# Row transfers of the scan stage: one merged transfer, or one per half of the partitions

## The chip, the cores and the metric

The kernel runs on one core of a Trainium2 chip, in one launch. The metric is the device time of the program in microseconds. Executions of the same kernel differ by some tenths of a per cent.

## What is computed

One step of a bidirectional diffusion backbone over 128 context and 1024 latent tokens of width 1024. The layer is a half-step SwiGLU network, a token mixer, and a second half-step SwiGLU network, each with norms and modulation around it. The mixer projects its input to r, k, v, a gate and the operands of a short convolution, runs an RWKV-7 scan (8 heads of 64) forward and backward, and merges the branches:

```
kk  = k * k_k;  kk = kk * rsqrt(sum_head(kk * kk))
k_d = k * (1 + (a_d - 1) * k_a)                      # one per direction d
S   = S * w_t + (S @ -kk_t) x (kk_t * a_t) + v_t x k_t
y_t = S @ r_t                                        # both directions are summed
bonus = sum_head(r * k_d * r_k)
out = merged(sigmoid(gates), y @ w_branch_a, conv @ w_branch_b) @ w_out
```

## The kernel before

All activations lie with features on the 128 partitions and 1152 tokens along the free axis, in three column tiles of 384. A float32 matmul is done as three products of rounded halves (hi and lo). The first SwiGLU network takes the time up to about 930 us, the mixer's scan stage reaches to about 2130 us, and the output projections and the second network come after it.

In the scan stage, heads are taken two at a time: a pair p has head 0 on partitions 0 to 63 and head 1 on partitions 64 to 127. Operands of the scan are kept in device memory in `ops2`, one tile for two pairs, of shape 128 partitions x 9 rows x 2 pairs x 1152 tokens; `opd[p]` is the part of pair p. The rows are read by the scan as five neighbours per direction in one transfer (`stage_b`, L1017, the tile ops). For this to give each engine its operands on the right partitions, some quantities lie in different rows for the two heads: k in rows 5 (head 0) and 4 (head 1), kk in rows 4 and 5, and the factors of k for the two directions in rows 2 and 1, and 7 and 6. The function `mirrored` (L772) builds the access pattern of such a quantity by hand, as two heads of 64 partitions with a step of one row between them, so that one transfer carries both.

Who uses it:

- `k_to_dram` (L778) stores each of the 12 projected k tiles, 128 x 384, 192 KB. Its `store` puts the transfer on a list that `stores` (L713) issues six dense steps later.
- `stage_k` (L943) runs 20 times, 16 for 256 columns and 4 for 128. It loads k (tile ok, L949), the two factors (tiles od and oi, L952 and L953), all merged, and r plainly (L1002). Then it makes kk (L971), with a sum of squares on PE (tile cps) and an inverse root of small DVE steps (tiles nx, ny, nt), stores kk merged (L972), and loads v and stores the bonus term (L962, L980, the tensor bvd).

All of these transfers, and the weight loads (`load_w`, L151, the tile wst), are issued by SP, one after another in the program's order; an issue that has to wait for something holds up what is behind it.

Three lanes of side work (`stage_k`, `stage_v`, `finish`) are advanced between the matmuls of the projections; priorities and a scheduler's estimates set the order on every engine. The scan itself goes by items: `stage_b` loads the operands and makes the products (tile scr on PE), `solve` inverts a triangular block on DVE (tiles un, tb, ys, xr; copies to ab), `step` advances the states. Each of the 18 items has such a solve.

Of the kernel before, what the change touches and what calls it, by code (L numbers as in the profile page):

```python
# [22 lines left out]
T = NCTX + NLAT  # L23
# [3 lines left out]
TW = T // NT  # L27
# [33 lines left out]
def body(ctx: ExitStack, tc: tile.TileContext, I: dict, y_prompt, y_sample, new_state):  # L61
# [393 lines left out]
    with ExitStack() as ph:  # L455
# [123 lines left out]
        later.add(x_rest())  # L579
        ffn(ap_, op_, sp, I["ffn1_w13"][0], I["ffn1_w2"][0], [(0,), (1,), (2,)], between, done, None, w0)  # L580
        mix = mixer(nc, tc, pool, locals())
        next(mix)
        later.flush()
# [75 lines left out]
def mixer(nc, tc, pool, env):  # L659
# [4 lines left out]
    V, G, S, PE, SP, I = e.V, e.G, e.S, e.PE, e.SP, e.I  # L664
# [3 lines left out]
    after, PB, later = e.after, e.PB, e.later  # L668
    ops2 = e.ops2
    opd, vd, bvd, gd, gad, gbd, yad, cbvd, xd = e.opd, e.vd, e.bvd, e.gd, e.gad, e.gbd, e.yad, e.cbvd, e.xd  # L670
# [38 lines left out]
    def store(dst, src):  # L709

        late.append((dst, src, clock["dense"]))
# [59 lines left out]

    def mirrored(p, row, sign, t0, n):  # L772

        t_ = ops2[p // 2]
        ps = 18 * T
        return bass.AP(tensor=t_.tensor, offset=t_.offset + 2 * row * T + p % 2 * T + t0, ap=[[64 * ps + 2 * sign * T, 2], [ps, 64], [1, n]])

    def k_to_dram(p):  # L778
        def f(t, ps):
            o = e.tmp("fso", tag="s")  # L780
            PB.first(S.activation(out=o, in_=ps, func=AF.Copy))
            store(mirrored(p, 5, -1, t * TW, TW), o)
        return f

    made = set()
# [14 lines left out]
    with ExitStack() as ph:  # L800
# [16 lines left out]
        HR = [slice(0, 64), slice(64, 128)]  # L817
# [125 lines left out]
        def stage_k(p, t0, n, bon=True):  # L943

            while ("rkv", p) not in made:
                yield 1
            nt = n // 128
            k = q1.tile([128, 256], F32, name="ok", tag="ok")[:, :n]
            PB.first(SP.dma_start(k, mirrored(p, 5, -1, t0, n)))  # L949
            r = oload(opd[p][:, 3], t0, n, "or")  # L950
            f0, f1 = (q1.tile([128, 256], F32, name=f"o{x}", tag=f"o{x}")[:, :n] for x in "di")
            SP.dma_start(f0, mirrored(p, 2, -1, t0, n))  # L952
            SP.dma_start(f1, mirrored(p, 7, -1, t0, n))  # L953
            yield GL
            a = q1.tile([128, 256], F32, name="oa", tag="oa")[:, :n]
            PB.first(S.activation(out=a, in_=k, func=AF.Square, scale=e.KK_[:, p:p + 1]))
            b = f0
            PB.first(V.tensor_tensor(out=b, in0=f0, in1=f1, op=ALU.add))
            V.tensor_tensor(out=b, in0=b, in1=k, op=ALU.mult)
            V.scalar_tensor_tensor(out=b, in0=r, scalar=rk4[:, p:p + 1], in1=b, op0=ALU.mult, op1=ALU.mult)  # L960
            v = r
            SP.dma_start(v, vd[p][:, t0:t0 + n])  # L962
            yield 3
            rs = compact(a, nt, sel, 2, 1.0, 1e-12, "oc", PB)
            yield GC
            ps = ps_.tile([128, 256], F32, name="kkb", tag="oc", bufs=1)[:, :n]
            for i in range(nt):
                for h in range(2):
                    PB.matmul(ps[HR[h], i * 128:(i + 1) * 128], rs[:, 2 * i + h:2 * i + h + 1].to_broadcast([128, 64]), ident, start=True, stop=True)
            kk = a  # L970
            V.scalar_tensor_tensor(out=kk, in0=k, scalar=e.KK_[:, p:p + 1], in1=ps, op0=ALU.mult, op1=ALU.mult)  # L971
            SP.dma_start(mirrored(p, 4, 1, t0, n), kk)  # L972
            made.add(("kk", p, (t0 - NCTX) // 256))
            yield 4
            ps = ps_.tile([128, 256], F32, name="bon", tag="oc", bufs=1)[:, :n]
            PB.matmul(ps, bones, b, start=True, stop=True)
            o = v
            V.tensor_tensor(out=o, in0=v, in1=ps, op=ALU.mult)
            S.activation(out=o, in_=o, func=AF.Identity, bias=gb4[:, p:p + 1])
            SP.dma_start(bvd[p][:, t0:t0 + n], o)  # L980
            yield GF

        def stage_v(p, t0, n, zv):


            nb = n // 64
            while ("rkv", p) not in made:
                yield 1
            v = oload(vd[p], t0, n, "lv", PB.first)
            yield GL  # L990
            ps = ps_.tile([128, 4, 64], F32, name="vt", tag="oc", bufs=1)
            for i in range(nb):
                for h in range(2):
                    hr, kr = HR[h], HR[1 - h]
                    PB.matmul(ps[kr, i], v[hr, i * 64:i * 64 + 64], cent[hr] if t0 >= NCTX else ident[hr, hr], start=True, stop=True)
            for h in range(2):
                S.activation(out=zv[HR[1 - h], 0:nb, p % 2, HR[h]], in_=ps[HR[1 - h], 0:nb], func=AF.Copy)
            made.add(("vt", p, (t0 - NCTX) // 256))

        def oload(src, t0, n, tag, first=lambda ins: None):  # L1000
            a = q1.tile([128, 256], F32, name=tag, tag=tag)[:, :n]
            first(SP.dma_start(a, src[:, t0:t0 + n]))  # L1002
            return a
# [327 lines left out]
        def ks(g, *bs):  # L1331
            return [("k", stage_k, 2 * g + pp, NCTX + b * 256, 256) for pp in range(2) for b in bs]

        def vs(g, *bs):
            return [("v", stage_v, 2 * g + pp, NCTX + b * 256, 256, ZV[zi(g, b)]) for b in bs for pp in range(2)]
# [4 lines left out]
        def kc(q):  # L1340
            return [("k", stage_k, 2 * q + pp, 0, 128) for pp in range(2)]

        def vc(q):
            return [("v", stage_v, 2 * q + pp, 0, 128, ZV[(0, 3)[q]]) for pp in range(2)]
# [90 lines left out]
    with ExitStack() as ph:  # L1435
# [47 lines left out]
        for t in range(NT):  # L1483
            xs = hx(t)
            for m in range(8):
                w = load_w(I["w_out"][0, :, m * 128:(m + 1) * 128], 8)
                ps = pd("po")
# [31 lines left out]
```

## Time and profile before

| | |
|---|---|
| median of 3 runs | 3277.09 us (3270.9 to 3281.26) |
| profiled execution | 3285.59 us, span 3283.8 us |
| mean granted TensorE clock | 0.951 |
| PE busy | 3023.5 us (92%) |
| DVE busy | 1817.5 us (55%) |
| ACT busy | 1150.9 us (35%) |
| queue of SP's transfers | 480248 packets, 326.79 MB, 33.4% of 16 engines |

The busy times and the queue are those of the profiled execution. A share of the DMA engines is a mean over all 16 of them: a transfer that uses two of them all the time gives some 0.13. The chain of waits is followed back from the last instruction, at each step to what released it; a piece of it that bears a transfer's name runs from the issue to the landing on which something waited.

### The profile page before, as it was taken

Reading aid. Unit: us, or ns where it says so; the run is one execution under the profiler, and the core shown is the slowest. Engines: PE = TensorE matmul, PEld = TensorE weight load, DVE = VectorE, ACT = ScalarE, POOL = GpSimd, SP = SyncE. Lnnn points to the kernel's source line nnn. Section 1 sums busy time; section 2 is a strip of 40 time slices with the busy share of each in tenths; the row PEclk is TensorE's granted clock in tenths of the full one; section 3 lists DMA queues with packets and bytes.
Section 4 is the critical chain, followed back from the end, with each engine's and each line's share of the span. In section 5 each row is a group of like instructions: output and inputs, shape, how many; then the busy total and the mean of one; then the engine's idle time right before and its main releaser. Section 6 shows DMA issues by size and latency. Waiting matters only on the chain.

```text
span 3283.8 us, 54891 instructions
## 1 busy us (share of the span) xinstructions
PE 3023.5 (92%) x21284; PEld 2850.2 (87%) x21284; DVE 1817.5 (55%) x4148; ACT 1150.9 (35%) x2618; POOL 454.6 (14%) x436
## 2 busy tenths in 40 slices
PE   8999999999989878888889898769989999999998
PEld 5999999999888867767777777649989999999998
DVE  7535665565875244557674667766683233323356
ACT  5421111114546224344544444422554211121244
POOL 1000000000240121333331323200120000000012
PEclk9999999999989988988999889869999999999999
DMA  8423333325534331322232333225532111111244
GB/s 270 144 63 95 97 102 87 86 85 153 157 109 162 125 118 58 110 76 78 81 111 84 98 87 98 85 78 157 178 104 87 36 46 43 44 39 42 82 144 132
DMA packets 481137, 330.78 MB, mean 101 GB/s; under 512 B 47008, under 2 KB 458988, under 8 KB 480876
## 3 DMA queue, kind: packets, MB, share of 16 engines
q1 hardware_dynamic: 480248, 326.79, 33.4%
q8 instruction: 167, 2.74, 0.3%
q14 instruction: 94, 0.77, 0.1%
q10 hardware_dynamic: 308, 0.44, 0.0%
q0 software_dynamic: 320, 0.04, 0.0%
HBM read 265.58 MB, written 61.60 MB: 100 GB/s over the span
## 4 chain that ended last, share of the span: by engine, by line
PE 68%; DVE 17%; DMA 6%; ACT 4%; issue 3%; POOL 1%; SPq 0%; DVEq 0%; ACTq 0%; POOLq 0%
PE po L220 6%; PE po L219 6%; PE po L221 6%; PE pg L220 5%; PE pg L219 5%; PE pg L221 5%; PE pu L220 5%; PE pu L219 5%; PE pu L221 5%; PE pj L740 3%; PE pj L742 2%; PE pj L741 2%; DVE un L1084 2%; PE scr L1043 2%; DMA ops<-opd 2%
## 5 line engine op out<-in xcount | busy, mean ns | idle before, releaser
L138 ACT ACTIVATE whi<-wst 128x512 fp32r<-128x512 f32 (+1 forms) x578 | 350.4, 611 | 753.1 <-PE po L221 392.8
L139 DVE TENSOR_TENSOR wlo<-wst,whi 128x512 fp32r<-128x512 f32 (+1 forms) x480 | 326.6, 681 | 305.2 <-ACT whi L138 295.7
L740 PE MATMUL pj<-hh,wlo 128*128 128x384 f32 x1056 | 382.2, 362 | 0.3 <-ACT fso L768 0.3
L741 PE MATMUL pj<-hl,whi 128*128 128x384 f32 x1056 | 372.7, 353 | 2.7 <-POOL hl L269 1.4
L742 PE MATMUL pj<-hh,whi 128*128 128x384 f32 x1056 | 374.6, 355 | 0.0
L219 PE MATMUL po<-ah,wlo 128*128 128x384 f32 x1056 | 357.1, 339 | 4.0 <-ACT ah L138 4.0
L220 PE MATMUL pg<-hl,whi 128*128 128x384 f32 x1056 | 356.1, 337 | 4.9 <-POOL hl L269 2.9
L219 PE MATMUL pg<-hh,wlo 128*128 128x384 f32 x1056 | 357.4, 338 | 1.7 <-DVE wlo L139 1.3
L220 PE MATMUL po<-al,whi 128*128 128x384 f32 x1056 | 356.3, 338 | 0.4 <-DVE al L139 0.4
L221 PE MATMUL po<-ah,whi 128*128 128x384 f32 x1056 | 355.7, 337 | 0.0
L221 PE MATMUL pg<-hh,whi 128*128 128x384 f32 x1056 | 355.5, 337 | 0.0
L219 PE MATMUL pu<-hh,wlo 128*128 128x384 f32 x1056 | 355.2, 336 | 0.0
L220 PE MATMUL pu<-hl,whi 128*128 128x384 f32 x1056 | 353.8, 335 | 0.0
L221 PE MATMUL pu<-hh,whi 128*128 128x384 f32 x1056 | 353.8, 335 | 0.0
L279 POOL TENSOR_TENSOR ss<-ss,sqt 128x384 f32<-128x384 f32 x78 | 88.7, 1140 | 1697.0 <-ACT sqt L278 1534.9
L432 DVE TENSOR_TENSOR sil<-sil,pu 128x384 f32<-128x384 f32 x132 | 72.9, 552 | 353.8 <-PE pu L221 353.6
L404 DVE TENSOR_TENSOR o<-o,po 128x384 f32<-128x384 f32 x288 | 159.2, 553 | 172.0 <-PE po L221 170.8
L740 PEld LDWEIGHTS pj<-hh,wlo 128*128 128x128 f32 x1056 | 206.4, 195 | 12.5 <-issue 7.0
L741 PEld LDWEIGHTS pj<-hl,whi 128*128 128x128 f32 x1056 | 207.1, 196 | 8.6 <-issue 2.2
L742 PEld LDWEIGHTS pj<-hh,whi 128*128 128x128 f32 x1056 | 206.9, 196 | 7.6 <-issue 3.7
L220 PEld LDWEIGHTS pg<-hl,whi 128*128 128x128 f32 x1056 | 199.9, 189 | 7.0 <-POOL hl L269 3.8
L219 PEld LDWEIGHTS po<-ah,wlo 128*128 128x128 f32 x1056 | 198.6, 188 | 5.0 <-ACT ah L138 5.0
(584 smaller groups left out, 5763.9 us busy)
## 6 DMA issues: line engine op xcount, KB each, us to landing
wst<-in_ffn_w SPq DMA_DIRECT2D x324, 256.0 KB
wmod<-in_w_mod SPq DMA_DIRECT2D x144, 256.0 KB
wst<-in_w_in SPq DMA_DIRECT2D x94, 256.0 KB
ops<-opd SPq DMA_DIRECT2D x36, 640.0 KB
wst<-in_ffn_w SPq DMA_DIRECT2D x96, 192.0 KB
xo<-xd SPq DMA_DIRECT2D x64, 192.0 KB
wst<-in_w_out SPq DMA_DIRECT2D x48, 256.0 KB
opd<-zv SPq DMA_DIRECT2D x24, 384.0 KB
```

What stands on the lines that cost most here:

```text
L138: first(S.activation(out=hi, in_=src, func=AF.Copy))
L139: eng.tensor_tensor(out=lo, in0=src, in1=hi.bitcast(F32), op=ALU.subtract)
L219: PE.matmul(ps, lo, xh, start=(k == 0), stop=False)
L220: PE.matmul(ps, hi, xl, start=False, stop=False)
L221: later.tick(PE.matmul(ps, hi, xh, start=False, stop=(k == nk - 1)))
L279: eng.tensor_tensor(out=ssum, in0=ssum, in1=q, op=ALU.add)
L404: V.tensor_tensor(out=O[m][t], in0=O[m][t], in1=ps, op=ALU.add)
L432: V.tensor_tensor(out=s, in0=s, in1=pu, op=ALU.mult)
L740: PE.matmul(ps, lo, xh, start=(k == 0), stop=False)
L741: PE.matmul(ps, hi, xl, start=False, stop=False)
L742: ins = PE.matmul(ps, hi, xh, start=False, stop=(k == 7))
L1043: PE.matmul(ps[64 * o:64 * o + 64, i], BK[64 * h:64 * h + 64, o, i * 64:i * 64 + 64], E[64 * h:64 * h + 64, s0 + i, h], start=True, stop=True)
```

## The change

`mirrored` returns two plain patterns, one per head, of 64 partitions and one row each. Each load and each store that used the merged pattern is issued twice, for the upper and the lower half of the tile. 80 transfers of `stage_k` and 12 of `k_to_dram` become 184. The computation stays.

```diff
--- before.py
+++ after.py
@@ -771,15 +771,14 @@
 
     def mirrored(p, row, sign, t0, n):
 
-        t_ = ops2[p // 2]
-        ps = 18 * T
-        return bass.AP(tensor=t_.tensor, offset=t_.offset + 2 * row * T + p % 2 * T + t0, ap=[[64 * ps + 2 * sign * T, 2], [ps, 64], [1, n]])
+        return [opd[p][64 * h:64 * h + 64, row + sign * h, t0:t0 + n] for h in range(2)]
 
     def k_to_dram(p):
         def f(t, ps):
             o = e.tmp("fso", tag="s")
             PB.first(S.activation(out=o, in_=ps, func=AF.Copy))
-            store(mirrored(p, 5, -1, t * TW, TW), o)
+            for h, dst in enumerate(mirrored(p, 5, -1, t * TW, TW)):
+                store(dst, o[64 * h:64 * h + 64])
         return f
 
     made = set()
@@ -946,11 +945,11 @@
                 yield 1
             nt = n // 128
             k = q1.tile([128, 256], F32, name="ok", tag="ok")[:, :n]
-            PB.first(SP.dma_start(k, mirrored(p, 5, -1, t0, n)))
+            turned(k, mirrored(p, 5, -1, t0, n), PB.first)
             r = oload(opd[p][:, 3], t0, n, "or")
             f0, f1 = (q1.tile([128, 256], F32, name=f"o{x}", tag=f"o{x}")[:, :n] for x in "di")
-            SP.dma_start(f0, mirrored(p, 2, -1, t0, n))
-            SP.dma_start(f1, mirrored(p, 7, -1, t0, n))
+            turned(f0, mirrored(p, 2, -1, t0, n))
+            turned(f1, mirrored(p, 7, -1, t0, n))
             yield GL
             a = q1.tile([128, 256], F32, name="oa", tag="oa")[:, :n]
             PB.first(S.activation(out=a, in_=k, func=AF.Square, scale=e.KK_[:, p:p + 1]))
@@ -969,7 +968,8 @@
                     PB.matmul(ps[HR[h], i * 128:(i + 1) * 128], rs[:, 2 * i + h:2 * i + h + 1].to_broadcast([128, 64]), ident, start=True, stop=True)
             kk = a
             V.scalar_tensor_tensor(out=kk, in0=k, scalar=e.KK_[:, p:p + 1], in1=ps, op0=ALU.mult, op1=ALU.mult)
-            SP.dma_start(mirrored(p, 4, 1, t0, n), kk)
+            for h, dst in enumerate(mirrored(p, 4, 1, t0, n)):
+                SP.dma_start(dst, kk[HR[h]])
             made.add(("kk", p, (t0 - NCTX) // 256))
             yield 4
             ps = ps_.tile([128, 256], F32, name="bon", tag="oc", bufs=1)[:, :n]
@@ -996,6 +996,10 @@
             for h in range(2):
                 S.activation(out=zv[HR[1 - h], 0:nb, p % 2, HR[h]], in_=ps[HR[1 - h], 0:nb], func=AF.Copy)
             made.add(("vt", p, (t0 - NCTX) // 256))
+
+        def turned(dst, srcs, first=lambda ins: None):
+            for h, src in enumerate(srcs):
+                first(SP.dma_start(dst[HR[h]], src))
 
         def oload(src, t0, n, tag, first=lambda ins: None):
             a = q1.tile([128, 256], F32, name=tag, tag=tag)[:, :n]
```

The scheduler places the other instructions anew. On SP, at the operands of the first item, the program of before has (lines of before; opd_110 is the tile of pairs 0 and 1, opd_111 that of pairs 2 and 3):

```order
L1234 DMA sti<-in_state_rwkv 128x2x64
L972 DMA opd_110<-oa 2x64x256
L716 DMA opd_111<-fso 2x64x384
L952 DMA od<-opd_110 128x1x256
L1017 DMA ops<-opd_110 128x10x128
L980 DMA bvd_117<-or 128x256
```

In the changed program the same place reads (L1021 is the former L1017, L1002 the loads in the new function `turned`, L1238 the former L1234):

```order
L1238 DMA sti<-in_state_rwkv 128x2x64
L716 DMA opd_111<-fso 64x384
L972 DMA opd_110<-oa 64x256 x2
L716 DMA opd_111<-fso 64x384 x2
L1002 DMA od<-opd_110 64x256 x2
L1021 DMA ops<-opd_110 128x10x128
L980 DMA bvd_117<-or 128x256
```

Each merged transfer is a pair there; halves of k stores stand on both sides of the kk pair, and the pair is still followed by the od load and the ops load.

On DVE, at the end of an early solve, the program of before has, from the first transpose of the solve to its two last copies (od is the bonus product, nx the start of the inverse root):

```order
L1104 STREAM_TRANSPOSE xr<-ys 128x256
L958 TENSOR_TENSOR od<-od,oi 128x256
L1105 STREAM_TRANSPOSE xr<-xr 128x256
L959 TENSOR_TENSOR od<-od,ok 128x256
L960 SCALAR_TENSOR_TENSOR od<-or,rk_9040,od 128x256
L1126 COPY ab_11542<-l64b 32x4x32
L1126 COPY ab_11543<-l64b 32x4x32
```

In the changed program, from the same transpose on:

```order
L1108 STREAM_TRANSPOSE xr<-ys 128x256
L958 TENSOR_TENSOR od<-od,ok 128x256
L1109 STREAM_TRANSPOSE xr<-xr 128x256
L959 SCALAR_TENSOR_TENSOR od<-or,rk_9040,od 128x256
L238 TENSOR_SCALAR nx<-cps 128x4
L229 TENSOR_SCALAR ny<-nx 128x4
L231 SCALAR_TENSOR_TENSOR nt<-ny 128x4
L232 TENSOR_TENSOR nt<-nt,nx 128x4
L233 SCALAR_TENSOR_TENSOR ny<-nt,ny 128x4
```

The copies to ab come after these rows and four more of the same root; at two more of the 18 solves rows of stage_k moved ahead of the copies in the same way.

## Rows read from the trace of the kernel before

**Rows 1.** Busy time by stage: us, busy us (instructions) per engine, clock, DMA share, GB/s.

```profile
0.00:930.00 930.00, 899.81 (x5097) 873.38 (x5098) 565.04 (x1078) 281.37 (x585) 58.89 (x61) 0.99 0.41 120
930.00:2130.00 1200.00, 1031.19 (x9727) 902.18 (x9727) 703.24 (x1954) 516.12 (x1336) 319.37 (x304) 0.91 0.33 100
2130.00:3283.80 1153.80, 1092.47 (x6468) 1074.63 (x6464) 549.23 (x1117) 353.40 (x698) 76.33 (x71) 0.96 0.29 86
```

**Rows 2.** Chain of waits from 930 to 2130 us: its shares by engine and line.

```profile
by line: PE pj L740 6.9%; PE pj L742 6.7%; PE pj L741 6.6%; issue 5.8%; DVE un L1084 5.7%; PE scr L1043 5.0%; DMA ops<-opd 4.6%; DMA opd<-oa 2.3%; DVE tb L1085 2.1%; DMA od<-opd 2.0%; DVE e L1036 1.9%; DMA bvd<-or 1.8%; PE sq L1161 1.7%; DV
```

**Rows 3.** Longest pieces of the whole chain: start us, us, what.

```profile
1077.28 6.95 DMA wst<-in_w_in
1085.31 9.49 DMA bvd<-or
1098.50 8.50 DMA wst<-in_w_in
1146.38 6.22 DMA opd<-oa
1152.62 8.49 DMA ops<-opd
...
1268.88 6.13 DMA lv<-vd
...
1307.57 5.86 DMA ok<-opd
...
1598.61 9.30 DMA od<-opd
1649.43 10.14 DMA od<-opd
```

**Rows 4.** Two pieces of the same chain with nothing in the way.

```profile
1000.80 2.70 DMA opd<-zv
...
1416.52 4.22 DMA ops<-opd
```

**Rows 5.** Stretches with one kind of transfer in flight; columns as in rows 1.

```profile
977.00:978.40 1.40, 1.40 (x10) 1.40 (x9) 1.10 (x1) 0.49 (x1) 0.02 (x1) 1.00 0.69 177
1150.00:1152.00 2.00, 2.00 (x14) 2.00 (x13) 0.00 (x0) 0.53 (x2) 1.91 (x2) 1.00 0.14 49
1657.50:1659.00 1.50, 1.50 (x11) 1.50 (x10) 1.43 (x3) 0.49 (x1) 0.00 (x0) 1.00 0.14 49
```

**Rows 6.** PE in order of time: start us, us, line, tiles; in brackets idle before.

```profile
1097.83 0.33 PE L740 MATMUL pj<-hh,wlo 128*128 128x384 f32 x1
1098.01 0.33 PE L741 MATMUL pj<-hl,whi 128*128 128x384 f32 x1
...
1107.59 1.01 PE L177 MATMUL cps<-cst,oa 128*128 128x2 f32 x4 [9.08 <-ACT oa L956]
...
1110.21 0.52 PE L742 MATMUL pj<-hh,whi 128*128 128x384 f32 x1
1110.53 0.52 PE L740 MATMUL pj<-hh,wlo 128*128 128x384 f32 x1
...
1163.61 0.69 PE L1043 MATMUL scr<-e,ops 64*64 64x128 f32 x4 [9.38 <-DVE ops L1032]
...
1609.66 0.32 PE L1112 MATMUL l<-xr,ab 32*32 32x32 f32 x4 [6.79 <-DVE nt L231]
```

**Rows 7.** SP's issues by source line: count, ns least/median/most, first and last start.

```profile
L972 SPq DMA_DIRECT2D opd<-oa x20: 492/517/533, 1081.8 to 2046.7; - x20
...
L1002 SPq DMA_DIRECT2D or<-opd x20: 319/329/464, 935.3 to 2014.7; - x20
...
L882 SPq DMA_DIRECT2D lw<-in_decay_w x2: 497/526/554, 975.7 to 982.9; - x2
...
L980 SPq DMA_DIRECT2D bvd<-or x20: 320/729/3842, 1085.3 to 2058.3; - x20
```

**Rows 8.** Waits of DVE, 930 to 2130 us: us in total, times, longest.

```profile
DVE nx L238 <- PE cps L177: 37.9, 20, 6.9
```


## Prediction

> **What bounds the kernel now.** I read the busy time by stage first, to see where an idle engine costs time [rows 1]. The kernel is matmul work: before 930 us PE is busy 899.81 of 930.00 us, after 2130 us 1092.47 of 1153.80. In between lies the scan stage, where every split transfer of the change stands, and there PE is busy 1031.19 of 1200.00 us: 169 us idle, more than in all the rest, and the granted clock is 0.91 against 0.99 and 0.96. PE's instructions stand in a fixed order, scan work and projections mixed, so the change can shorten the kernel only by shortening these waits (or by giving clock back).
>
> Then I read the chain of waits in that stage [rows 2]. Four names of transfers stand in its line: ops<-opd 4.6%, opd<-oa 2.3%, od<-opd 2.0%, bvd<-or 1.8% of 1200 us, so 55.2, 27.6, 24.0 and 21.6 us. opd<-oa is the merged kk store, od<-opd a merged load. The other two are plain transfers that run behind merged ones. The longest pieces of the chain say the same [rows 3]: a merged load of 128 KB takes 9.30 or 10.14 us, a merged store of 128 KB 6.22 us, plain transfers queued behind them 9.49 (bvd), 8.49 (ops) and 6.95 and 8.50 us (wst). Where nothing is in the way, the plain store opd<-zv of 384 KB takes 2.70 us and the 640 KB load of ops 4.22 us [rows 4].
>
> Why a merged transfer is slow is told by the share of the 16 DMA engines [rows 5]. From 1150 to 1152 us one merged od load moves alone: the share is 0.14, some two engines of sixteen, at 49 GB/s, and from 1657.5 to 1659 us again 0.14 and 49 GB/s. At that rate 128 KB take 2.7 us and the 192 KB of a k store 4.0 us. From 977.0 to 978.4 us the 64-partition loads of lora weights (L882, L883) move: share 0.69, 177 GB/s. So 64 rows are no hindrance to using most of the engines; the merged form is. 64 merged transfers of 128 KB, 16 of 64 KB and 12 of 192 KB keep these two engines busy for 64 x 2.7 + 16 x 1.3 + 12 x 4.0 = 242 us, and every other transfer has a part on them and lands only when that part does.
>
> The Trainium skill gives the same reading in "DMA: Bandwidth & Descriptors", "Why a DMA increments its semaphore by 16 and not by 1": the number of engines is the largest up to 16 that divides the slowest dimension of both patterns. By that rule the merged pattern, whose slowest dimension is 2, gets 2 engines and a half of 64 rows gets 16; the trace agrees for the merged form (0.14) and nearly for the 64-row loads (0.69).
>
> **The change part by part.** 20 rounds of stage_k (16 of 256 columns, 4 of 128) issue 4 merged transfers each, and 12 k stores stand beside them: 92 transfers become 184. The bytes stay.
>
> *Landing times.* I price each piece of the chain at what the same or a larger transfer takes when nothing is in the way, plus the issue of the second half (0.33 us, below) for the split ones. ops, 10 pieces: 55.2 - 10 x 4.22 = 13.0. kk store, 5 pieces: 27.6 - 5 x 3.03 = 12.5. od, 3 pieces: 24.0 - 3 x 3.03 = 14.9. bvd, 3 pieces: 21.6 - 3 x 2.70 = 13.5. The two wst pieces at no less than ops: 15.45 - 8.44 = 7.0. lv 6.13 - 2.70 = 3.4, ok 5.86 - 3.03 = 2.8 [rows 2 to 4]. Together 67 us of the chain.
>
> *How much of that PE feels.* Four places can be followed [rows 3, 6]. At 1107.59 us PE resumes after 9.08 us; bvd and wst would give 6.8 + 4.3 there, so the whole 9.0. At 1163.61 us it resumes after 9.38; kk store and ops give 3.2 + 4.3 = 7.5. At 1609.66 us after 6.79; od gives 6.3. But behind the longest piece, the od load of 1649.43 us, PE is busy 1.50 of 1.50 us between 1657.5 and 1659 [rows 5]: projections fill it, and the 7.1 us there buy nothing. So 22.8 of 32.0 us are felt, 71%. I take that share for the stage: 47 us.
>
> *SP's issue time.* A merged transfer costs SP 0.517 us to issue, a plain one of 128 rows and 256 columns 0.329, and the trace has no 64-row transfer of plain form; the 64-row load L882, whose rows are in four pieces, takes 0.526 [rows 7]. A half has one run per row like the plain one, so I take 0.33; then a pair costs 0.66 - 0.517 = 0.14 more, 13 us over 92. With 0.526 it is 0.54 more, 49 us. Against it, bvd's store, which stands behind a merged transfer, takes 0.729 in the median and up to 3.842 us to issue, where 0.32 is its least: some 8 us of SP over its 20 issues that should come back. SP mostly waits for data, so I put 5 us of the added issue on the path. Lower end: nothing, if the returned issue time outweighs it; upper end: half of 49, 24 us.
>
> *Order.* On SP the halves stand as pairs where the merged one stood, and the kk pair is still directly ahead of the od pair and the ops load. What is queued behind a waiting half is the same as before, plus the other half. On DVE the order moved at three of 18 solves: there some eight rows more of stage_k's inverse root (from nx on) stand between the solve's transposes and its last copies (ab<-l64b), and nx waits for PE 37.9 us over 20 times, 1.9 us each [rows 8]. Three such waits ahead of a solve's end: 6 us. Lower bound 0, where the solve is late anyway.
>
> *Sum.* -47 + 5 + 6 = -36 us. The profiled execution took 3285.6 us (span 3283.8 and 1.8 around it), 8.5 above the median of the runs shown, 3277.1; I take the difference to that median: 3241 us. Left out on purpose: clock. Before the gap at 1107.59 us matmuls follow each other by 0.18 us, after it by 0.32, half the clock, 1.2 instead of 2.4 GHz [rows 6]. Shorter gaps might save some of that, 8 us at most (about 1.5 us at each of five or so long gaps).
>
> **The rivals.**
>
> *The whole chain is felt.* What the projections fill now is run earlier, so the end moves by all 67 us plus the 8 of clock: -75, 3202 us. For it: these pieces are on the path that sets the end, and behind ops, the name with most pieces, stands scr, at which PE's order stops until it has come [rows 6]. Against: PE busy behind the 10.14 us piece.
>
> *Hidden anyway.* The solve's DVE chain and the inverse roots are next late at most places, and only the two gaps above 9 us shrink by half: -8, 3269 us. For it: nx and its like wait for PE themselves. Against: PE's gaps at three followed places begin and end with a transfer.
>
> *Slower, by SP's queue.* SP issues in order, and in a round four pairs stand ahead of the ops and weight loads. If a half costs 0.526 us to issue and lands no sooner than now, each round delays what is behind it by 4 x 0.54 = 2.2 us, 44 us over 20 rounds; half on the path and the 6 of DVE: +28, 3305 us. It decides from the point at which a half's issue exceeds 0.5 us and the store of kk still takes 5 us to land.
>
> The Trainium skill speaks for this side in "DMA: Bandwidth & Descriptors", "Rules for kernel authors": transfers to disjoint partition halves aren't worth while, since both spread over the same 16 engines and serialize, and one transfer of 128 partitions is to be used. By that rule nothing is won and the added issues are lost, so the sum would be the third rival's. The rule supposes that the one transfer uses all engines, and the shares of 0.14 contradict that here.
>
> *It does not do what it says.* A half keeps to few engines, or a merged pattern is rebuilt when the program is put together: landing stays, 13 us of issue half felt: +7, 3284 us. Against: the 64-row loads at 0.69.
>
> **How the numbers follow.** My forecast gets 0.58, the whole chain 0.12, hidden 0.14, slower by the queue 0.11, no effect 0.05. About 0.3%, 10 us, is what a measurement of this kernel can tell from no change. Faster by more than that: 0.58 + 0.12 and a third of hidden, 0.75. Within: the rest of hidden and half of no effect, 0.12. Slower: 0.13. The range reaches from the whole chain (3204) to just beyond no change (3281), and leaves most of the third rival out. Faster cases alone lie between 3204 and 3267.
>
> **What would show it.** Right: stretches in which a split transfer moves alone show a share far above 0.14; the chain's pieces od<-opd and opd<-oa are near 3 us, bvd's issue near 0.33 in the median; PE's gaps at the first ops load and the first ok load fall below 4 us; PE's idle time between 930 and the end of the scan falls from 169 to some 130 us. The step from chain to PE is wrong if the pieces shrink and PE's idle does not; the price of SP is wrong if a half takes 0.5 us to issue. The forecast fails if landing times stay, or if the waits of DVE on PE (nx, scr) grow by what the transfers gave.

## The result, and the profile after

The changed kernel takes 3231.12 us in the median of 4 runs (3226.22 to 3234.37), the kernel before 3277.81 beside it: ratio 0.9859, interval 0.9838 to 0.988. That is 46.7 us less; the forecast was 3241 us, 36 less. The profiled execution took 3226.22 us (span 3224.3), the fastest of the four, so the two traces differ by 59.5 us of span, more than the medians do.

By stage of the changed kernel, with the columns of [rows 1]; the stage that ended at 2130 us before now ends at about 2070:

```profile
0.00:930.00 930.00, 899.35 (x5089) 871.07 (x5090) 565.01 (x1078) 280.86 (x584) 58.98 (x61) 0.99 0.40 120
...
930.00:2070.00 1140.00, 1014.23 (x9753) 891.06 (x9753) 708.28 (x1954) 516.88 (x1336) 318.53 (x304) 0.94 0.35 105
2070.00:3224.30 1154.30, 1091.59 (x6450) 1074.17 (x6446) 548.47 (x1117) 353.94 (x698) 76.26 (x71) 0.96 0.29 86
```

The first stage and the last are as long as before. The middle one is 60 us shorter, in two parts: PE's idle time falls from 168.8 to 125.8 us, 43 less, and its busy time from 1031.19 to 1014.23, 17 less for about the same 9,700 matmuls, with the granted clock at 0.94 in place of 0.91 [rows 1].

The chain of waits of the changed kernel from 930 to 2080 us, its shares and its longest pieces (start us, us, what):

```profile
by line: PE pj L742 7.5%; PE pj L741 7.4%; PE pj L740 7.4%; issue 7.4%; DVE un L1088 6.7%; PE scr L1047 4.8%; DMA ops<-opd 3.7%; DVE e L1040 2.3%; DVE tb L1089 2.1%; ACT e L1051 2.1%; POOL e L1052 2.0%; DVE e L1039 1.9%; PE sq L1165 1.7%; D
...
1140.97 4.83 DMA ops<-opd
1174.16 5.87 DMA ops<-opd
1190.60 4.37 DMA ops<-opd
...
1389.03 12.06 issue
```

Of the four transfers in [rows 2] only ops is left with a share to see, and its pieces, 4.37 to 5.87 us here, are nearer the 4.22 us of an undisturbed one [rows 4]. bvd, lv, ok and od, at 6 to 10 us in [rows 3], are no longer among the longest; DVE's solve (un) has gone from 5.7% to 6.7%, "issue" from 5.8% to 7.4%.

What waited for a landing, 930 to 2130 us (us in total, times, longest us): first the kernel before, rows not shown so far, then the changed one, where the window takes in 60 us of the next stage.

```profile
POOL ops L1031 <- DMA ops<-opd: 94.8, 20, 17.2
DVE e L1035 <- DMA ops<-opd: 46.7, 8, 12.2
DVE od L958 <- DMA od<-opd: 28.8, 7, 6.2
ACT whi L138 <- DMA wst<-in_w_in: 27.0, 15, 12.6
```

```profile
DVE nx L238 <- PE cps L177: 56.4, 20, 8.3
...
POOL ops L1035 <- DMA ops<-opd: 40.2, 16, 8.7
...
DVE e L1039 <- DMA ops<-opd: 26.8, 8, 6.7
...
ACT whi L138 <- DMA wst<-in_w_in: 4.6, 7, 2.3
```

POOL waits less than half as long for ops, and ACT's wait for weights falls from 27.0 to 4.6 us. Neither ops nor wst was edited: these are the transfers behind the merged ones. In their place DVE waits longer for PE, 56.4 us against 37.9 [rows 8].

SP's issues by source line in the changed kernel (L1002 the loads, L972 the store of kk, L980 bvd), with the line on landing of L1002 and of L972:

```profile
L1002 SPq DMA_DIRECT2D ok<-opd x40: 450/588/1972, 951.1 to 1935.9; - x40
L1002 SPq DMA_DIRECT2D od<-opd x40: 444/544/677, 1008.3 to 1955.2; - x40
...
DMA to landing us min/median/max: 1.9/2.2/4.7
...
L972 SPq DMA_DIRECT2D opd<-oa x40: 452/524/659, 1083.9 to 1986.1; - x40
...
DMA to landing us min/median/max: 1.8/1.9/4.6
...
L980 SPq DMA_DIRECT2D bvd<-or x20: 325/532/2945, 1087.3 to 1991.5; - x20
```

A half takes SP 0.52 to 0.59 us, as much as a merged transfer did [rows 7], and lands after some 2 us.

Halves of the changed kernel that move alone: the two of a kk store, with the stretch between them and the busiest tenth of a microsecond of the first, and one of a load of od (columns as in rows 1). Then PE at its first ops load, with its idle time before in brackets:

```profile
1711.90:1712.40 0.50, 0.50 (x9) 0.43 (x5) 0.47 (x3) 0.49 (x3) 0.00 (x0) 1.00 0.55 131
1712.10:1712.20 0.10, 0.10 (x1) 0.10 (x2) 0.10 (x1) 0.09 (x2) 0.00 (x0) 1.00 1.01 236
1712.40:1712.60 0.20, 0.20 (x3) 0.20 (x2) 0.17 (x2) 0.20 (x3) 0.00 (x0) 1.00 0.01 0
1712.60:1713.10 0.50, 0.50 (x9) 0.25 (x9) 0.47 (x3) 0.47 (x3) 0.00 (x0) 1.00 0.54 131
...
1485.50:1486.00 0.50, 0.04 (x1) 0.00 (x0) 0.47 (x3) 0.47 (x3) 0.23 (x1) 1.00 0.42 131
```

```profile
1148.30 0.53 PE L1047 MATMUL scr<-e,ops 64*64 64x128 f32 x4 [2.39 <-DVE ops L1036]
```

A half of 64 KB moves in 0.5 us at 131 GB/s, where a merged transfer has 49 GB/s [rows 5]. Its share is 0.42 to 0.55 over that time against 0.14, and 1.01, all the engines, at its busiest. The halves of a pair go one after the other, with 0.2 us between them in which nothing moves. The gap of 9.38 us is 2.39 [rows 6].

### The profile page after: what moved, and what is told of

Its sections match the earlier page's. It is cut to its first block, busy times and chain, and to the rows that moved or that the text cites. A ratio compares the mean times of both kernels' runs of the same rounds, so it can differ in the third digit from the quotient of the medians.

```text
span 3224.3 us, 55042 instructions
## 1 busy us (share of the span) xinstructions
PE 3005.2 (93%) x21284; PEld 2836.3 (88%) x21284; DVE 1821.8 (57%) x4148; ACT 1151.7 (36%) x2618; POOL 453.8 (14%) x436
## 4 chain that ended last, share of the span: by engine, by line
PE 69%; DVE 17%; ACT 5%; issue 4%; DMA 3%; POOL 1%; SPq 0%; DVEq 0%; ACTq 0%; POOLq 0%
PE po L220 6%; PE po L219 6%; PE po L221 6%; PE pg L220 5%; PE pg L219 5%; PE pg L221 5%; PE pu L220 5%; PE pu L219 5%; PE pu L221 5%; PE pj L742 3%; PE pj L740 3%; PE pj L741 3%; DVE un L1088 2%; PE scr L1047 2%; DMA ops<-opd 1%
## 5 line engine op out<-in xcount | busy, mean ns | idle before, releaser
L740 PE MATMUL pj<-hh,wlo 128*128 128x384 f32 x1056 | 375.4, 355 | 0.3 <-ACT fso L768 0.3
```

The lines of the kernel that those rows point to most:

```text
L740: PE.matmul(ps, lo, xh, start=(k == 0), stop=False)
```

## Experiments

The theory: a merged transfer uses two engines of sixteen and lands late, and what is behind it lands late with it; the shorter landings gave the time. The rivals: the other order of the instructions gave it; the added issues on SP are felt and hide part of the gain; only the landing of the split transfers counts, not the traffic behind them. Each kernel was timed in five rounds beside the kernel before; "changed" is 3231.12 us, ratio 0.9859.

**e1: one plain transfer, the order of before.** Both heads are read and written in the same row, so the second head's operands are others, and k is scaled by 0.05 for it (the edit is against the kernel before). On PE, DVE, ACT and POOL the instructions stand as in the kernel before, and there are 92 transfers as there.

```diff
-        t_ = ops2[p // 2]
-        ps = 18 * T
-        return bass.AP(...)
+        return opd[p][:, row, t0:t0 + n]
...
-            PB.first(S.activation(out=o, in_=ps, func=AF.Copy))
+            PB.first(S.activation(out=o, in_=ps, func=AF.Copy, scale=0.05))
```

> The kernel before, but every row transfer reads or writes one plain row for both heads (128 partitions, one transfer), so that the second head's operands come from the wrong row; k is scaled by 0.05 so that the scan stays bounded. The order on PE, DVE, ACT and POOL is that of before, row for row; there are 92 row transfers, not 184. Theory 1 (two-engine landing): stretches in which one such transfer moves alone show a DMA share far above 0.14, issues cost about 0.33 us, and the time falls at least as far as with the split, since no second halves are issued: 3215 us, 3200 to 3230. Theory 2 (the new order gave the gain): the order is the old one, so 3278 us within 5.

3217.86 us, ratio 0.9819 (0.9804 to 0.9835). SP's issue and landing of od (L950) in this kernel, and DVE's wait for PE:

```profile
L950 SPq DMA_DIRECT2D od<-opd x20: 319/320/502, 1007.9 to 1951.6; - x20
...
DMA to landing us min/median/max: 2.0/2.1/3.9
...
DVE nx L238 <- PE cps L177: 53.2, 23, 8.2
```

With the old order the whole gain is there and 13 us more: the pattern made the gain, and the order didn't. And nx waits 53.2 us in the order of before, so that wait can grow without a change of order.

**e2: halves as two blocks of 32 rows.** Meant to put the halves back on two engines.

```diff
+        ... ap=[[32 * ps, 2], [ps, 32], [1, n]]) for h in range(2)]
```

> The changed kernel, but each half of 64 partitions is written as 2 x 32, so that its slowest dimension is 2. Order on all five engines as in the changed kernel, row for row, with the same 184 transfers. Theory 1: DMA share of a half alone near 0.14 again, landings of 4 to 9 us, and the time goes back to that of before or beyond it, since the added issues (92 at 0.5 us, 50 us of SP) stay: 3295 us, 3275 to 3310. Theory 2 (order): 3231 us within 8.

3232.96 us, 0.9865 (0.985 to 0.9879), and the loads land as in the changed kernel:

```profile
DMA to landing us min/median/max: 2.0/2.2/4.8
```

Two blocks that follow each other without a step are the same rows as one of 64, and it behaved as one. So it tells nothing on two engines; it stands as a repeat of the changed kernel.

**e3, e4 and e11: one part alone.** In e3 only the 12 k stores are split, in e4 only the 60 loads, in e11 only the 20 kk stores; the others are merged as before. e3 has the order of before on PE, DVE, ACT and POOL. e4 and e11 have orders of their own there, so their times hold an unknown part of the order. The edit of e4:

```diff
-            for h, dst in enumerate(mirrored(p, 5, -1, t * TW, TW)):
-                store(dst, o[64 * h:64 * h + 64])
+            store(merged(p, 5, -1, t * TW, TW), o)
...
-            for h, dst in enumerate(mirrored(p, 4, 1, t0, n)):
-                SP.dma_start(dst, kk[HR[h]])
+            SP.dma_start(merged(p, 4, 1, t0, n), kk)
```

> Only the 12 k stores are split, loads and kk stores stay merged; the order on PE, DVE, ACT and POOL is that of before. Theory 1: they hold 48 of the 242 us in which two engines are busy with merged transfers, and little waits for them directly: 3268 us, 3258 to 3276. Rival (the early jam between 1077 and 1165 us comes from the k stores, 12 of which stand there): the two PE gaps of 9 us shrink to under 4 and the time falls by 15 or more, to 3263 or less.

3264.05 us, 0.9958 (0.9945 to 0.9972): 14 us. PE's longest gap left at the two early places is the one at ops:

```profile
1146.79 0.69 PE L1052 MATMUL scr<-e,ops 64*64 64x128 f32 x4 [5.12 <-DVE ops L1041]
```

So the rival of this run is right about the first gap: 9.08 us before [rows 6], it is gone with the k stores split alone. The second falls only to 5.12 us, and the 15 us that it asked for are not quite there.

> Only the 60 loads (k and the two factors) are split, the kk and k stores stay merged. Theory 1: the loads hold 60% of the two engines' time, but 60 added issues of 0.5 us stand against it: 3255 us, 3240 to 3268. Rival (the kk store ahead of the ops load is what the chain feels): od and ok leave the chain, opd<-oa stays at 4 us or more, and the time falls by 10 at most: 3268 or more.

3239.86 us, 0.9892 (0.9876 to 0.9909): 38 us, more than was expected. The rival's kk store stays on the chain, but not its 10 us at most.

> Only the kk stores are split, loads and k stores stay merged. Theory C: 48 of the 242 us of the two engines go, as with the k stores alone (13 us): 3263 us, 3255 to 3270. Theory D: the five kk stores on the chain shrink from 5.4 to 2 us each and the ops loads start sooner: 3257 us or less.

3256.17 us, 0.9933 (0.9919 to 0.9947): 20 us, which lies in the ranges of both theories and parts nothing. The three alone make 72 us, together 46.7. In e4 the kk store is still on the chain:

```profile
1136.13 5.17 DMA opd<-oa
1141.36 6.24 DMA ops<-opd
1172.61 4.79 DMA opd<-oa
```

With the loads out of its way it takes 5.17, not 6.22 us [rows 3]. In e11, with loads and k stores left merged, bvd, wst and ops are as late as before, and so is PE's first gap:

```profile
1085.05 9.46 DMA bvd<-or
1096.12 10.11 DMA wst<-in_w_in
1151.22 8.65 DMA ops<-opd
```

```profile
1107.40 1.01 PE L177 MATMUL cps<-cst,oa 128*128 128x2 f32 x4 [9.06 <-ACT oa L960]
```

Each part gives time to the others' landings as well as its own, so two parts can win the same time. That fits parts that don't add up; it isn't shown by itself, and the orders of e4 and e11 may have a share in it.

**e5 and e6: the order of the changed kernel, other engine counts.** The loads stay halves, but a half is read as two blocks of 32 rows (e5) or eight of 8 (e6) that overlap by one row, so part of the operands are others. Both have the order of the changed kernel on every engine, SP too.

```diff
+        ... ap=[[31 * ps, 2], [ps, 32], [1, n]]) for h in range(2)]     # e5
+        ... ap=[[7 * ps, 8], [ps, 8], [1, n]]) for h in range(2)]       # e6
```

> The changed kernel with the loads of k and of the two factors alone written so that a half's slowest dimension is 2: two blocks of 32 partitions with a step of 31 partitions between them, which can't be joined to one of 64 (the second block reads one partition too low, so the operands of stage_k are partly wrong). Order as in the changed kernel on every engine, row for row, and as many transfers. Theory 1 (number of engines): a load alone shows a DMA share near 0.14, its landing takes 4 us or more, and what splitting the loads alone gave, 38 us, is lost again: 3265 us, 3250 to 3285. Theory 2 (order): 3232 us within 8.

3241.97 us, 0.9903 (0.9886 to 0.9919).

> As the run with two, but eight blocks of 8 partitions with a step of 7, slowest dimension 8 (again partly wrong operands). Theory 1: eight engines carry a half, a load alone shows a share near 0.5 or is too short to be seen, landings are those of the changed kernel plus 0.2 us: 3234 us, 3226 to 3244. Rival (any pattern of three dimensions is slow, whatever its first count): as with two, 3250 us or more.

3228.46 us, 0.9861 (0.9846 to 0.9876), the same as the changed kernel. So it isn't the third dimension of the pattern but the number of blocks. A load of od that moves alone in e5 shows it directly (columns as in rows 1); in the changed kernel the same load has 0.42 and 131 GB/s, above:

```profile
1495.00:1496.00 1.00, 1.00 (x30) 0.97 (x32) 1.00 (x5) 0.97 (x4) 1.00 (x2) 1.00 0.13 46
```

e5 loses only some 10 us (14 by the ratios) where 34 were expected, and lies outside both ranges written down for it: with the stores split, loads on two engines cost that much and no more. Its pieces on the chain are later than the changed kernel's, and DVE's wait for nx is that of before.

```profile
1138.08 6.47 DMA ops<-opd
...
1246.25 6.18 DMA od<-opd
...
DVE nx L238 <- PE cps L177: 38.1, 19, 8.1
```

The wait of nx is back at 38.1 us in the changed kernel's own order: with e1 this shows that it goes with the landings, and not with the order. By the Trainium skill, "DMA: Bandwidth & Descriptors", "Why a DMA increments its semaphore by 16 and not by 1", two blocks go to two engines and eight to eight; that e5 is slower and e6 isn't agrees, as do the 0.13 above and the 0.14 of [rows 5].

**e7: quarters.** 368 transfers of 32 partitions, 184 issues more than in the changed kernel.

```diff
-        return [opd[p][64 * h:64 * h + 64, row + sign * h, t0:t0 + n] for h in range(2)]
+        return [opd[p][32 * i:32 * i + 32, row + sign * (i // 2), t0:t0 + n] for i in range(4)]
...
```

> The changed kernel with four transfers of 32 partitions where two of 64 stand, 368 in all; the scheduler places some rows anew. Theory A (SP's issues cost, the 13 us between plain rows in one transfer and halves are theirs): 184 more issues at 0.5 us are 92 us of SP, and by the same share felt (13 us for 92 x 0.7 us = 64 us) 19 us are felt: 3251 us, 3242 to 3270. Theory B (issues are hidden, the 13 us are the order): 3231 us within 8.

3224.27 us, 0.9846 (0.9831 to 0.9861). SP's issue of a quarter and its landing:

```profile
L1002 SPq DMA_DIRECT2D od<-opd x80: 302/420/1540, 1007.5 to 1958.0; - x80
...
DMA to landing us min/median/max: 1.5/1.8/5.9
```

Four quarters take SP 1.68 us in place of 1.09 for two halves, and nothing is lost. That SP's issues are felt falls, with one reserve: the instructions stand in an order of their own here, and a quarter lands in 1.8 us in place of 2.2, either of which could have won back what the issues cost.

**e8: fewer issues.** The two factors lie in one tile, and one transfer per half brings both: 144 transfers.

```diff
...
-            turned(f0, mirrored(p, 2, -1, t0, n))
-            turned(f1, mirrored(p, 7, -1, t0, n))
+            turned(fs_, [opd[p][64 * h:64 * h + 64, 2 - h:8 - h:5, t0:t0 + n] for h in range(2)])
```

> The changed kernel, but the two factors lie in one tile, and one transfer per half loads both rows of a head (step of five rows): 144 transfers, 40 fewer. The prefetch of the second factor ahead of the first is lost. Theory A (issues felt by a fifth): 40 x 0.55 = 22 us of SP less, 3227 us, 3219 to 3233. Theory B (hidden): 3231 us within 5; 3240 or more if the lost prefetch decides.

3227.7 us, 0.9851 (0.9837 to 0.9866): 40 issues fewer give no more than a run can tell, in an order of its own and within the ranges of both theories.

**e9 and e10: idle stores.** Behind each pair of the changed kernel SP issues one more store of a constant, into memory that nobody reads: in e9 in the merged form, in e10 of the same size in plain form. The two have the same order on PE, DVE, ACT and POOL, and on SP.

```diff
+        after(SP.dma_start(bass.AP(... ap=[[64 * 3 * n + n, 2], [3 * n, 64], [1, n]]), e.cst[:, 0:n]), ins)   # e9
+        after(SP.dma_start(j[:, 0], e.cst[:, 0:n]), ins)                                                      # e10
```

> The changed kernel, and behind each pair of halves one more store of the same size in the merged form, from constants to a place in device memory of its own that nobody reads or waits for: 92 more transfers that put the two engines' 242 us back, while the row transfers themselves stay split. Theory C (what the merged form costs is mostly the traffic behind it, which has a part on the two engines): bvd, ops and wst are late again, 3260 us, 3250 to 3280. Theory D (it was mostly the merged transfers' own landing): the same time as the run with plain extra stores, within 8 us. Order on PE, DVE, ACT and POOL is the same in these two runs.

3251.69 us, 0.9912 (0.9891 to 0.9932).

> As the run before, but each extra store is a plain one of 128 partitions: 92 more issues of some 0.35 us and as many more bytes, on all engines. Both theories: 3234 us, 3224 to 3244. If issues or the order cost more than thought, 3245 or more; the two runs are then compared with each other alone.

3225.41 us, 0.9843 (0.9827 to 0.9859), no slower than the changed kernel, with 92 more issues (in an order of its own again) and as many bytes as e9. The longest pieces of the chain, e9 first, then e10:

```profile
1099.57 7.17 DMA opd<-fso
1106.74 8.27 DMA vd<-fso
1120.47 6.16 DMA bvd<-or
1129.26 6.19 DMA wst<-in_w_in
1145.69 5.67 DMA opd<-oa
1151.44 5.29 DMA ops<-opd
```

```profile
1141.30 4.81 DMA ops<-opd
1173.13 5.71 DMA ops<-opd
```

Nobody waits for an idle store, and in merged form they still cost 26 us by the medians (10 to 34 by the ends of the two intervals; the six executions of e9 reach from 3238 to 3256 us) against the same bytes in plain form: what is behind them lands late, bvd and wst at some 6 us where [rows 3] has 7 to 9.5, and other stores at 7 to 8. SP's issue time isn't the cause, since an idle store takes it 0.539 us in merged form and 0.577 in plain form, in the median. So the traffic behind 92 merged transfers is worth about half of the 46.7 us by itself.

That the rest is their own landing is concluded from this, not measured; e4's kk stores, still at 4.79 and 5.17 us on the chain, fit it. The two can't be parted cleanly, because merged transfers also stand behind each other. Before the od piece of 9.30 us in [rows 3], SP had issued two more of 128 KB in merged form:

```profile
1596.55 0.52 SPq L972 DMA_DIRECT2D opd<-oa  x1
1597.12 0.50 SPq L949 DMA_DIRECT2D ok<-opd  x1
1598.61 0.48 SPq L952 DMA_DIRECT2D od<-opd  x1
```

At 49 GB/s [rows 5] the three need 8.0 us (an estimate), and the third landed at 1607.91, 11.4 us after the first was issued. So most of its 9.30 us is waiting for the other two.

**e12: one tile for both factors, in quarters.** e7 and e8 together, 288 transfers.

> Four transfers of 32 partitions each, the two factors loaded together (step of five rows): 288 transfers. The two runs of its parts stand at 3224 and 3228 us. If quarters land sooner than halves and fewer issues help a little: 3222 us, 3214 to 3230. If both are noise around the changed kernel: 3229 us within 6.

3221.0 us (3216.25 to 3226.66), 0.9829 (0.9813 to 0.9845): faster than the kernel before by 55 us, and ahead of the changed kernel by about 0.3%. The intervals just meet with the changed kernel's, and don't with that of its repeat e2; the order of the instructions is another one too, so what the 0.3% come from isn't shown.

## Why the prediction was right

The sign, the mechanism and nearly the size were right: 3231 against 3241 us. By its own steps:

- **Landing times: right.** Priced at 67 us of the chain. ops went from 55.2 us to 42.6 (3.7% of 1150 us), 12.6 less where 13.0 was priced, with pieces of 4.1 to 5.9 us; od, bvd, lv and ok are gone from the longest pieces, and the kk store takes 2.04 us in the one piece left (at 1711.38 us). That the plain transfers were late because of the merged ones was argued from two shares; e9 against e10 shows it. One of the two shares was misread: from 1150 to 1152 us the od load did not move alone, as the kk store, issued at 1146.38 us and landed at 1152.60, and a k store, issued at 1147.29, were under way too. All of them are merged, so two engines and 49 GB/s stand, for the merged transfers together. The sign that was asked for, a half's share far above 0.14, came with 0.42 to 0.55.
- **What PE feels of it: right in the traces.** 71% of 67 us, 47, was put down; PE's idle time fell by 43, to 126 us where "some 130" was written. The 9.08 us gap is gone, the one at ops 2.39 us.
- **SP's issue: wrong price, right that little is felt.** A half was put at 0.33 us like a plain row transfer; it takes 0.52 to 0.59, so a pair adds some 0.57 us and the 92 pairs 52 us of SP, a little above the 49 that the dearer price gave. Of this 5 us were charged and nothing can be seen: 184 issues more in e7 and 92 more in e10 don't slow the kernel, and 40 fewer in e8 don't speed it up. bvd's issue fell to 0.532 us, not to 0.33.
- **Order on DVE: not seen.** 6 us were charged for nx standing ahead of the solve's last copies. nx's wait grew by 18.5 us, but not by the order (e1, e5), and far less than POOL's and DVE's waits for ops fell, by 74.5 us; DVE's wait for scr went from 106.7 to 104.4 us. So the sign of failure that the prediction named for these waits did not come. Whether order costs part of the 13 us between e1 and the changed kernel stays open: e1 also has half as many transfers and another k, and e10, at 7.6 us from e1, has an order that is neither's.
- **Clock: left out, and worth about what was set aside.** "8 us at most" was written. In the two traces the stage's busy time fell by 17 us at 0.94 in place of 0.91, but the profiled execution of before, at a mean granted clock of 0.951, lies near the slow end of its kernel. The 29 executions of the kernel before that were timed beside the experiments go from 0.950 (3286.86 us) to 0.958 (3270.57 us), 0.955 in the mean, and the four of the changed kernel from 0.959 to 0.962. At 16.3 us for 0.008, the rise of 0.0055 goes with some 11 us of the 46.7 (an estimate, and clock and gaps move together, so it proves no cause).

The two charges that cost nothing, 5 and 6 us, and a clock of 8 to 11 us make about 20, and the forecast was 10 us short. So by the medians the 47 us of the landing times would be some 10 too many, which made up for half of what was missing: that the number came so near is in part luck. The profiled pair, 59.5 us apart, would leave only 4 too many; the share of each is known to some 10 us only.

Of the rivals, slower by SP's queue had its first condition, a half's issue above 0.5 us, and not its second, a kk store still at 5 us. The Trainium skill's rule against splitting into partition halves ("DMA: Bandwidth & Descriptors", "Rules for kernel authors") didn't decide here, since the one transfer it prefers moved on two engines. The halves do go one after the other, as it says, though SP also issues them 0.5 us apart, and each is over in 0.5 us. The whole chain felt (3202 us) was too much: what came next, nx on PE and DVE's solve, took its part. The piece "issue" of 12.06 us is not new; it took 13.86 us before.

## What to carry to other kernels

Look at the share of the DMA engines while one transfer moves alone: one at 0.14 can cost as much in the transfers behind it as in its own landing, and the chain of waits shows the victims, not the cause. Here two transfers on all engines beat one on two, with a queue that had time to spare; a full queue was not tried. Before pricing the added issues, ask whether that queue ever delays anything: here 184 more of them could not be seen in the time. And before a sum is made from one trace, see where its execution lies among the others of the kernel: at 0.951 this one was near the slow end.

## What was not expected of the hardware

A load of 64 rows of 1 KB takes SP longer to issue than one of 128 rows in the same place: 0.54 to 0.59 us in the median and 0.444 at its least, against 0.320 and 0.319 in e1. One of 32 rows takes 0.42, with 0.30 at its least, and halves that read eight blocks of 8 rows take 0.59 to 0.61. The number of rows isn't all of it: the idle stores of 128 rows in e10 take 0.577 in the median, with 0.338 at their least. What sets this no run here tells.

A half of a kk store reaches a share of 1.01, but for some 0.1 us: in half a microsecond it is over, at a mean share of 0.55, and 0.2 us follow in which nothing moves. A window of 0.4 us that takes in the pause shows a share of 0.33 and 82 GB/s and hides this; a tenth of a microsecond shows it.
